# A two-layer hybrid model on one core: tokens by their place in chunks of four, u by block transposes, S5 states as the stationary operand

## The chip, the cores and the metric

One core of a Trainium2 chip runs the whole program; seven are idle. The metric is device time in microseconds of one execution, from 1187.76 us (median of three) for the kernel before. The engines meant below are TensorE (PE, with its weight loads PEld), VectorE (DVE), ScalarE (ACT), GpSimd (POOL) and SyncE (SP), whose queue issues the transfers.

## What is computed

Two layers over 256 tokens of width 1024, float32. Each layer is a half-weighted SwiGLU feed-forward, a mixing stage, and a second feed-forward:

```python
for l in range(DEPTH):
    x = x + 0.5 * swiglu(rms_norm(x, norm_ffn1[l]), ffn1_wi[l], ffn1_wo[l])
    h = rms_norm(x, norm_mix[l])
    (u, q_raw, k_cmp, v_cmp, k_sel, v_sel, k_win, v_win,
     nsa_gate, gate_a, gate_b) = jnp.split(h @ w_in[l], SPLIT_POINTS, axis=-1)
    y_a = s5_branch(u, ...)
    y_b = nsa_branch(q_raw, k_cmp, ...) @ nsa_w_up[l]
    merged = jax.nn.sigmoid(gate_a) * y_a + jax.nn.sigmoid(gate_b) * y_b
    x = x + merged @ w_out[l]
    x = x + 0.5 * swiglu(rms_norm(x, norm_ffn2[l]), ffn2_wi[l], ffn2_wo[l])
```

`s5_branch` is a complex linear recurrence over time in 32 groups of 64 states with 16 inputs and outputs each, then a gelu and a gated projection. `nsa_branch` is attention with eight heads in two key groups, over keys that are compressed (windows of 32 tokens, step 16, through a small network), selected and local; at 256 tokens all blocks are selected.

## The kernel before

Tokens stand on the partitions, 128 in each of two tiles t. The float32 weights come through a ring of four `raw` buffers on SP's queue, in the order of `plan`; ACT rounds each chunk to a high part `whi` (L157, L337), DVE computes the rest `wlo` (L158, L337), and PE multiplies three times for each product (`mm3`, L369 to L371: high by high, high by low, low by high). `gemm` does this for 128x512, 384 or 408 columns, chunk by chunk for both tiles; its results are the tiles `gu`. The smaller products are plain float32.

The mixing stage (`mix`) computes u (512 columns of w_in), then 384 columns (`kvT`, part of the keys), 408 columns (more keys, values, gates), the compression of keys and values (`compress`), q, and the gate columns. Beside it runs a generator, `s5_main`, which `pull` advances by a budget whenever `next` fetches a chunk; `attn_units` follows in it. S5 works in chunks of four tokens: U4 holds for each pair of groups the inputs of a chunk, 4 places × 32 channels on the partitions and 64 chunks along the free axis. Products with G (L538, through `mm_cols`) give each chunk's contribution, `rotate` and a scan (L885, DVE) run the recurrence over 64 chunks and leave the states `Sp`, and L903 adds K·U4 and the two C·Sp to the output, which is passed through gelu (L907) and split.

U4 is made like this: u is evicted by ACT (L1271), turned by four PE transposes per tile (L1274), copied out of PSUM (L1275, ACT) into `uT`, and rearranged by sixteen copies of 32 partitions, half on ACT (L868), half on DVE (L870). The weights of the compression stand in `raw` without a split and are the stationary operand; its input `kc2` is read with a step of eight (L538 from `compress`); POOL fills `kc2` (L530, `gcopy`). The compressed key is normalized and rotated on ACT, DVE and POOL between L1091 (its product) and L1096 (`kb`), which PE transposes at L1103.

The order of the instructions on each engine is written by a scheduler at build time, with its own estimates of durations; `issue_after` and `keep_in_program_order` bind some of it. Engines take their instructions strictly in that order.

The kernel's last step (`finish`, L381) adds each half tile of y to x on DVE and stores it with one transfer of SP's queue.

Of the kernel before, what the change touches and what calls it, by code (L numbers as in the profile page):

```python
# [8 lines left out]
F32R = mybir.dt.float32r  # L9
BF = mybir.dt.bfloat16  # L10
AF = mybir.ActivationFunctionType
# [22 lines left out]


def shape_constants():
    a = np.zeros((128, 128 + CONST_W), np.float32)
    a[:, :128] = np.eye(128)
# [12 lines left out]

    c, s = cs(np.arange(SEQ))
    put('cos', c.reshape(2, 128, 64).transpose(1, 0, 2))
    put('sin', s.reshape(2, 128, 64).transpose(1, 0, 2))
# [6 lines left out]
    put('any', (t >= 31).astype(np.float32).reshape(2, 128).T)  # L61
# [7 lines left out]
    put('caus', np.where(r[None, :] > r[:, None], np.float32(-1e30), np.float32(0)).astype(np.float32))  # L69
    cm = np.where((cend[None, :] <= t[:, None]) & (n[None, :] < 15), np.float32(0), np.float32(-1e30))  # L70
    put('cmask', cm.reshape(2, 128, 16).transpose(1, 0, 2).astype(np.float32))
    return a


class Model:
# [32 lines left out]
    def add(k, ap, split=True, g=None):  # L108

        k.chunks.append((ap, split, g))  # L110

    def load(k, o, i):
# [743 lines left out]

    def s5_main(k, uT):

        nc, P = k.nc, k.P
        V, S = nc.vector, nc.scalar  # L860
        r4 = lambda dt=F32: k.sb([128, 1024], "r4", k.opt['n4'], dt)
        U4 = r4().rearrange("p (a j) -> p a j", a=16)
        for q in range(4):
            for u in range(4):
                o = U4[u * 32:(u + 1) * 32].rearrange("p (a q) j -> p q a j", q=4)[:, q]
                i = uT[q * 32:(q + 1) * 32].rearrange("p a (j u) -> p u a j", u=4)[:, u]
                if u % 2 == 0:
# [23 lines left out]
        for h in range(2):  # L891
            yield from k.rotate(Sp, Z, P['cs'], P['sn'], slice(h * 8, h * 8 + 8), -1)
        yt = r4().rearrange("p (a t s) -> p a t s", a=4, s=4)
# [15 lines left out]
        yh, yl = r4(F32R), r4(F32R)  # L909
        k.split(yt.rearrange("p a t s -> p (a t s)"), yh, yl)  # L910
        k.yT = [t.rearrange("p (a t) -> p a t", a=4) for t in (yh, yl)]
        yield 1.0

# [41 lines left out]
    def nsa_prep(k, l):  # L955
# [21 lines left out]
        N['cg'], N['sg'], N['cc'] = cg, sg, cc  # L977
        kc2 = k.sb([128, 2, 3, 128], "kc2", 1)
        nc.gpsimd.memset(kc2[:, :, 2], 0.0)
        bk = k.bank((128, 32))  # L980
        nc.tensor.transpose(bk, N['pe'], k.id[:32, :32])
        V.tensor_copy(kc2[:, :, 2, 0:16], bk.rearrange("p (a b) -> p a b", a=2))
        N['kc2'] = kc2
# [84 lines left out]
    def compress(k, kvT):  # L1068
# [4 lines left out]
        for kv in range(2):  # L1073
            for h in range(2):
                for a in range(2):
                    i = kvT[h * 64:(h + 1) * 64, kv].rearrange("p (j a) -> p a j", a=2)[:, a]
                    k.gcopy(kc2[a * 64:(a + 1) * 64, kv, h], i)
        hid = k.sb([128, 2, 2, 16], "hid", 1)
        nc.gpsimd.memset(hid[:, :, :, 15:16], 0.0)
        for kv in range(2):  # L1080
            ps = k.bank((128, 3, 15), 'ya')
            for m in range(16):
                if m % 8 == 0:
                    w = k.next().rearrange("p (m c) -> p m c", m=8)
                k.mm_cols(ps, [(w[:, m % 8], kc2[:, kv, :, m:m + 113:8])], m == 0, m == 15)
            pb = k.sb([128, 1], "pb", 2)
            V.tensor_copy(pb, ps[:, 2, 0:1])
            S.activation(hid[:, kv, :, 0:15], ps[:, 0:2], AF.Gelu_apprx_tanh, bias=pb)

# [162 lines left out]
    def mix(k):  # L1252
# [15 lines left out]
        uT = r4().rearrange("p (a t) -> p a t", a=4)  # L1268
# [154 lines left out]
```

## Time and profile before

| what | value |
|---|---|
| median of three runs (lowest, highest) | 1187.76 us (1186.48, 1188.71) |
| the profiled execution | 1188.25 us |
| its span | 1186.4 us |
| PE busy | 1161.3 us (98%), 6724 instructions |
| DVE, ACT, POOL busy | 839.6, 674.6, 231.8 us |
| mean granted clock | 0.996 of 2.4 GHz |

The span runs from the first to the last instruction; the execution's own time adds what lies around it. A busy PE is not PE at its peak: matmuls overlap, a 128x512 one is shown with some 0.39 us and the next begins about 0.23 us later. So unit prices are taken from the starts of successive rows, not from the durations shown.

### The profile page before, as it was taken

To read this page: it belongs to the slowest core of one execution; us is meant where nothing else is said; L and a number is where in the kernel's file an instruction comes from. 1 tells how busy PE (TensorE), PEld (TensorE's weight loads), DVE (VectorE), ACT (ScalarE), POOL (GpSimd) and SP (SyncE) were. 2 spreads that over 40 slices of the span, in tenths; PEclk is the share of its full clock that TensorE was granted. 3 is DMA by queue.
4 is the path that set the end of the run, shared out by engine and by line. 5 is a ranking of instruction groups with operands and counts; after the bars stand their busy time and mean duration, and the time that the engine had idled before them with its cause. 6 is when DMAs were issued, how large, how long until landed. Compare 5 with 4: busy or idle time off the path is not lost. (4 is left out here: it accounts for less than half of the span.)

```text
span 1186.4 us, 18796 instructions
## 1 busy us (share of the span) xinstructions
PE 1161.3 (98%) x6724; PEld 944.9 (80%) x6724; DVE 839.6 (71%) x1494; ACT 674.6 (57%) x1176; POOL 231.8 (20%) x285
## 2 busy tenths in 40 slices
PE   9999999999999999999999999999999999999998
PEld 6888777887877888888888887778778778888886
DVE  5797979586875755555667987886878756655554
ACT  6655554745765565554566555546657646655552
POOL 3002654044032000000030043711341310000000
PEclk9999999999999999999999999999999999999999
DMA  8766555364443566565565656445635435665662
GB/s 237 226 194 184 170 154 179 105 192 144 145 140 104 165 211 187 185 190 183 187 188 178 195 162 182 142 152 155 199 107 173 129 107 160 214 185 188 188 185 89
DMA packets 150078, 200.48 MB, mean 169 GB/s; under 512 B 9952, under 2 KB 120832, under 8 KB 149984
## 3 DMA queue, kind: packets, MB, share of 16 engines
q1 hardware_dynamic: 148848, 197.46, 54.3%
q0 software_dynamic: 1136, 1.82, 0.9%
q8 instruction: 53, 0.87, 0.3%
q14 instruction: 41, 0.34, 0.1%
HBM read 198.18 MB, written 1.05 MB: 168 GB/s over the span
## 5 line engine op out<-in xcount | busy, mean ns | idle before, releaser
L158 DVE SCALAR_TENSOR_TENSOR wlo<-raw,gcol,whi 128x512 fp32r<-128x512 f32 (+2 forms) x480 | 359.0, 785 | 110.0 <-ACT whi L157 107.6
L157 ACT ACTIVATE whi<-raw,gcol 128x512 fp32r<-128x512 f32 (+2 forms) x480 | 316.1, 710 | 193.0 <-PE gu L370 92.4
L369 PE MATMUL gu<-whi,hh 128*128 128x512 f32 (+2 forms) x944 | 372.2, 394 | 0.6 <-ACT whi L157 0.6
L371 PE MATMUL gu<-wlo,hh 128*128 128x512 f32 (+2 forms) x944 | 369.1, 396 | 2.3 <-DVE wlo L158 2.3
L370 PE MATMUL gu<-whi,hl 128*128 128x512 f32 (+2 forms) x944 | 368.9, 391 | 0.0
L337 DVE TENSOR_TENSOR wlo<-raw,whi 128x1024 fp32r<-128x1024 f32 x128 | 160.9, 1259 | 103.1 <-ACT whi L337 101.1
L337 ACT CAST whi<-raw 128x1024 fp32r<-128x1024 f32 x128 | 134.5, 1053 | 135.4 <-PE gu L370 112.1
L371 PEld LDWEIGHTS gu<-wlo,hh 128*128 128x128 f32 x944 | 177.8, 189 | 37.8 <-DVE wlo L158 2.6
L370 PEld LDWEIGHTS gu<-whi,hl 128*128 128x128 f32 x944 | 178.2, 189 | 35.2
L369 PEld LDWEIGHTS gu<-whi,hh 128*128 128x128 f32 x944 | 178.3, 189 | 34.5 <-ACT whi L157 0.8
L344 POOL TENSOR_SCALAR rs<-ss 128x1 f32<-128x1 f32 (+3 forms) x22 | 7.2, 328 | 378.4 <-ACT w2k L351 351.6
L370 PE MATMUL yb<-whi,w1k 128*128 128x512 f32 x176 | 71.4, 406 | 0.7 <-DVE w1k L337 0.7
L371 PE MATMUL yb<-wlo,w1k 128*128 128x512 f32 x176 | 69.2, 393 | 0.0
L369 PE MATMUL yb<-whi,w1k 128*128 128x512 f32 x176 | 69.0, 395 | 0.0
L370 PE MATMUL ya<-whi,w1k 128*128 128x512 f32 x176 | 68.8, 391 | 0.0
L371 PE MATMUL ya<-wlo,w1k 128*128 128x512 f32 x176 | 68.7, 391 | 0.0
L369 PE MATMUL ya<-whi,w1k 128*128 128x512 f32 x176 | 68.2, 393 | 0.0
L1207 POOL TENSOR_SCALAR w2k<-w2k,sm 128x128 f32<-128x128 f32 (+1 forms) x64 | 38.9, 629 | 100.6 <-ACT w2k L1191 63.2
L337 ACT CAST w1k<-tr 128x256 fp32r<-128x256 f32 x88 | 32.5, 370 | 45.7 <-PE tr L484 45.7
L501 DVE SCALAR_TENSOR_TENSOR w1k<-gu,rs,w1k 128x256 f32<-128x256 f32 x88 | 42.0, 479 | 16.2 <-ACT w1k L500 16.2
L500 ACT ACTIVATE w1k<-gu,rs 128x256 f32<-128x256 f32 x88 | 40.9, 467 | 20.0 <-PE gu L371 13.7
L337 DVE TENSOR_TENSOR w1k<-tr,w1k 128x256 fp32r<-128x256 f32 x88 | 36.7, 418 | 10.1 <-ACT w1k L337 10.0
(316 smaller groups left out, 1502.1 us busy)
## 6 DMA issues: line engine op xcount, KB each, us to landing
raw<-in_ffn_wi_dram SPq DMA_DIRECT2D x352, 256.0 KB, 3.3
raw<-in_ffn_wo_dram SPq DMA_DIRECT2D x88, 512.0 KB, 3.6
raw<-in_w_in_dram SPq DMA_DIRECT2D x48, 512.0 KB, 4.5
raw<-in_ssm_w_glu_dram SPq DMA_DIRECT2D x32, 256.0 KB, 3.4
raw<-in_w_out_dram SPq DMA_DIRECT2D x16, 512.0 KB, 3.3
raw<-in_cmp_w_dram SPq DMA_DIRECT2D x8, 512.0 KB, 4.8
raw<-in_nsa_w_up_dram SPq DMA_DIRECT2D x16, 256.0 KB, 4.1
raw<-in_w_in_dram SPq DMA_DIRECT2D x8, 408.0 KB, 4.2
```

Of the source, the lines that this page charges most:

```text
L157: k.hi_ins[i] = k.nc.scalar.activation(hi[:, s], r[:, s], AF.Copy, scale=c)
L158: k.lo_ins = k.nc.vector.scalar_tensor_tensor(lo[:, s], r[:, s], c, hi[:, s].bitcast(F32), op0=ALU.mult, op1=ALU.subtract)
L337: return k.nc.scalar.copy(hi, src), k.nc.vector.tensor_sub(lo, src, hi.bitcast(F32))
L344: k.nc.gpsimd.tensor_scalar(a, ss, scale, EPS, op0=ALU.mult, op1=ALU.add)
L369: mm(ps, a[0], b[0], start=first, stop=False)
L370: mm(ps, a[1], b[0], start=False, stop=False)
L371: return mm(ps, a[0], b[1], start=False, stop=last)
L500: m = nc.scalar.activation(sg, ps[t][:, :256], AF.Silu, scale=r[t])
L501: nc.vector.scalar_tensor_tensor(a, ps[t][:, 256:], r[t], sg, op0=ALU.mult, op1=ALU.mult)
L1207: G.tensor_scalar(w[:, i], p[:, i], cf[:, j:j + 1], 0.0, op0=ALU.mult, op1=ALU.add)
```

## The change

The host lays the tokens of each tile of 128 out by their place in a chunk of four: partition p holds token 4 (p mod 32) + p div 32. Tables and masks are laid out likewise, and the output is stored back in four transfers per half tile, two on SP's queue and two on ACT's. U4 then comes from u by 32x32 block transposes on DVE, one for each tile (L1280 of the changed kernel). The last step of S5 takes the states and U4 as the stationary operand and K and C as the moving one; its output has chunks on the partitions and is transposed back by PE after the gelu (L913). `kc2` is laid out with the eight offsets outermost, and its 33 columns (16 and 16 windows, and the offset's one) are read in order.

```diff
+PLACE = 4 * (np.arange(128) % 32) + np.arange(128) // 32
...
+    def store(k, t, h, xs):
+
+        for u in range(4):
+            o = bass.AP(tensor=k.out.tensor, offset=k.out.offset + (t * 128 + u) * D + h * 512,
+                        ap=[[4 * D, 32], [1, 512]])
+            (k.nc.sync if u % 2 else k.nc.scalar).dma_start(o, xs[u * 32:(u + 1) * 32])
...
-                    k.nc.sync.dma_start(k.out[0, t * 128:(t + 1) * 128, h * 512:(h + 1) * 512], xs)
+                    k.store(t, h, xs)
...
-    def s5_main(k, uT):
+    def s5_main(k, U4):
...
-        U4 = r4().rearrange("p (a j) -> p a j", a=16)
-        for q in range(4):
-            for u in range(4):
-                o = U4[u * 32:(u + 1) * 32].rearrange("p (a q) j -> p q a j", q=4)[:, q]
-                i = uT[q * 32:(q + 1) * 32].rearrange("p a (j u) -> p u a j", u=4)[:, u]
-                if u % 2 == 0:
-                    S.copy(o, i)
-                else:
-                    V.tensor_copy(o, i)
-            yield 0.7
...
-        T = ((P['K'], U4), (P['C'][0], Sp[0]), (P['C'][1], Sp[1]))
+        yh, yl = r4(F32R), r4(F32R)
+
+        T = ((U4, P['K']), (Sp[0], P['C'][0]), (Sp[1], P['C'][1]))
         for h in range(2):
-            bk = k.bank((128, 2, 4, 64), 'yb')
-            for i, (m, v) in enumerate(T):
-                for a in range(2):
-                    for s in range(4):
-                        for q in range(4):
-                            p = h * 8 + a * 4 + q
-                            nc.tensor.matmul(bk[q * 32:(q + 1) * 32, a, s], m[:, p, s * 32:(s + 1) * 32], v[:, p],
-                                             start=(i == 0 and a == 0 and s == 0), stop=(i == 2),
-                                             skip_group_check=True)
-                    yield 0.4
-            S.activation(yt[:, h * 2:h * 2 + 2].rearrange("p a t s -> p a s t"), bk, AF.Gelu_apprx_tanh)
+            bk = k.bank((128, 4, 128), 'yb')
+            for q in range(4):
+                for i, (v, m) in enumerate(T):
+                    for e in range(2):
+                        p = (2 * h + e) * 4 + q
+                        nc.tensor.matmul(bk[e * 64:(e + 1) * 64, q], v[:, p], m[:, p], start=(q == 0 and i == 0),
+                                         stop=(i == 2), skip_group_check=True)
+                yield 0.6
+            g = k.sb([128, 4, 4, 32], "w2k", k.opt['n2'])
+            S.activation(g.rearrange("p s q c -> p q s c"), bk.rearrange("p q (s c) -> p q s c", s=4),
+                         AF.Gelu_apprx_tanh)
             yield 0.6
...
+            bk = k.bank((128, 4, 128))
+            for s in range(4):
+                nc.tensor.transpose(bk[:, s], g[:, s].rearrange("p q c -> p (q c)"), k.id)
+            o = [y.rearrange("p (a s j) -> p s a j", a=8, s=4)[:, :, 4 * h:4 * h + 4] for y in (yh, yl)]
+            k.split(bk.rearrange("p s (a j) -> p s a j", a=4), *o)
...
-                    i = kvT[h * 64:(h + 1) * 64, kv].rearrange("p (j a) -> p a j", a=2)[:, a]
-                    k.gcopy(kc2[a * 64:(a + 1) * 64, kv, h], i)
+                    i = kvT[h * 64:(h + 1) * 64, kv].rearrange("p (n m a) -> p a m n", m=8, a=2)[:, a]
+                    k.gcopy(kc2[a * 64:(a + 1) * 64, kv, :, h * 16:(h + 1) * 16], i)
...
-            ps = k.bank((128, 3, 15), 'ya')
+            ps = k.bank((128, 33), 'ya')
...
-                k.mm_cols(ps, [(w[:, m % 8], kc2[:, kv, :, m:m + 113:8])], m == 0, m == 15)
+                k.mm_cols(ps, [(w[:, m % 8], kc2[:, kv, m % 8, m // 8:m // 8 + 33])], m == 0, m == 15)
...
-            u = k.sb([128, 512], "w2k", k.opt['n2'])
-            S.activation(u, ps[t], AF.Copy, scale=k.r[t])
-            bk = k.bank((128, 4, 128))
-            for i in range(4):
-                nc.tensor.transpose(bk[:, i], u[:, i * 128:(i + 1) * 128], k.id)
-            S.copy(uT[:, :, t * 128:(t + 1) * 128], bk)
-        k.bg, k.budget = k.s5_main(uT), k.opt['B1']
+            u = k.sb([128, 16, 32], "w2k", k.opt['n2'])
+            S.activation(u.rearrange("p a c -> p (a c)"), ps[t], AF.Copy, scale=k.r[t])
+            V.transpose(U4[:, :, t * 32:(t + 1) * 32], u)
+        k.bg, k.budget = k.s5_main(U4), k.opt['B1']
...
-            S.copy(kvT[:, :, t * 128:(t + 1) * 128], bk)
+            for i in range(2):
+                S.copy(kvT[:, i, t * 128:(t + 1) * 128].rearrange("p (j u) -> p u j", u=4),
+                       bk[:, i].rearrange("p (u j) -> p u j", u=4))
```

In the changed kernel most lines stand 5 to 13 lower: L538 becomes L550, L903 L904, L907 L908, L1091 L1098, L1096 L1103, L1103 L1110. The scheduler's order changes in the two mixing stages alone, but for the copies that fill `kc2`'s last column. Three places of layer 1 follow.

ACT from the eviction of u's first half (L1271 before, L1279 now) to the eviction of the 384-column product (L1282 before). Before:

```order
L1271 ACTIVATE w2k<-gu,rs 128x512
L157 ACTIVATE whi<-raw,gcol 128x384 x4
L1271 ACTIVATE w2k<-gu,rs 128x512
L1275 COPY r_8212<-tr 128x4x128 x2
L868 COPY r_8239<-r_8212 32x4x64 x6
L157 ACTIVATE whi<-raw,gcol 128x408 x2
L868 COPY r_8239<-r_8212 32x4x64 x2
L157 ACTIVATE whi<-raw,gcol 128x408 x4
```

Now:

```order
L1279 ACTIVATE w2k<-gu,rs 128x512
L169 ACTIVATE whi<-raw,gcol 128x384 x4
L1279 ACTIVATE w2k<-gu,rs 128x512
L169 ACTIVATE whi<-raw,gcol 128x408 x6
L1287 ACTIVATE w1k<-gu,rs 128x256
L1289 ACTIVATE kp<-gu,rs 128x128
```

All copies between the second half of u and the 408-column splits are gone.

PE at the compression of layer 1 (`kc` is its input). Of the names before, r_8239 is U4 and r_7571 is K; of those of the change, r_8056 is U4, r_8522 and r_8523 are the two Sp, r_7415 is K, r_7427 and r_7428 are the two C. The last name of a pair is the stationary operand. Before:

```order
L538 MATMUL yb<-r_8239,r_7376 64x64 x15
L538 MATMUL ya<-kc_7745,raw 64x45 x64
L903 MATMUL yb<-r_8239,r_7571 32x64 x9
L369 MATMUL gu<-whi,hh 128x512
L370 MATMUL gu<-whi,hl 128x512
L369 MATMUL gu<-whi,hh 128x512
L370 MATMUL gu<-whi,hl 128x512
L903 MATMUL yb<-r_8239,r_7571 32x64 x26
```

Now:

```order
L550 MATMUL ya<-kc_7589,raw 64x33 x64
L904 MATMUL yb<-r_7415,r_8056 64x128 x2
L904 MATMUL yb<-r_7427,r_8522 64x128 x2
L904 MATMUL yb<-r_7415,r_8056 64x128
L904 MATMUL yb<-r_7428,r_8523 64x128 x2
L904 MATMUL yb<-r_7415,r_8056 64x128
L381 MATMUL gu<-whi,hh 128x512
L382 MATMUL gu<-whi,hl 128x512
L381 MATMUL gu<-whi,hh 128x512
L382 MATMUL gu<-whi,hl 128x512
L904 MATMUL yb<-r_7415,r_8056 64x128
L904 MATMUL yb<-r_7427,r_8522 64x128 x2
```

Before, K·U4 alone stood here, and the products with Sp only 48 gemm matmuls later; now products with both Sp stand ahead of q's first gemm matmuls.

DVE at the compressed key (kc, then kb) of layer 1. Before:

```order
L997 TENSOR_TENSOR nr_8678<-tr,rs 32x64
L999 TENSOR_TENSOR nr_8680<-nr_8678,cc 32x64
L158 SCALAR_TENSOR_TENSOR wlo<-raw,gcol,whi 128x512 x2
L1059 TENSOR_TENSOR w2k<-w2k,rs 128x512
L1005 TENSOR_TENSOR kc<-nr_8680,nr_8681 32x64
L158 SCALAR_TENSOR_TENSOR wlo<-raw,gcol,whi 128x512 x2
L1061 TENSOR_TENSOR w2k<-w2k,cg 128x512
L1096 COPY kb<-kc 32x128
L158 SCALAR_TENSOR_TENSOR wlo<-raw,gcol,whi 128x512 x3
```

Now:

```order
L1004 TENSOR_TENSOR nr_8500<-tr,rs 32x64
L1006 TENSOR_TENSOR nr_8502<-nr_8500,cc 32x64
L349 TENSOR_TENSOR kT<-tr,kT 64x2x128
L1066 TENSOR_TENSOR w2k<-w2k,rs 128x512
L1012 TENSOR_TENSOR kc<-nr_8502,nr_8503 32x64
L1068 TENSOR_TENSOR w2k<-w2k,cg 128x512
L1103 COPY kb<-kc 32x128
L1119 TENSOR_TENSOR vc<-tr,cst 128x512
L349 TENSOR_TENSOR kct<-tr,kct 128x2x16
L1073 TENSOR_TENSOR w2k<-w2k 128x4x64 x2
```

Two splits between kc and kb are gone, and of the two ahead of kc as well. On PE, 24 gemm matmuls stood between the products L1091 and the transpose L1103 that needs kb; now 24 stand between L1098 and L1110 in layer 0, and 20 in layer 1, with nine and three matmuls of L904 beside them.

## Rows read from the trace of the kernel before

**Rows 1.** part 1 of the page, busy time, share of the span and instructions of each engine

```profile
PE 1161.3 (98%) x6724; PEld 944.9 (80%) x6724; DVE 839.6 (71%) x1494; ACT 674.6 (57%) x1176; POOL 231.8 (20%) x285
```

**Rows 2.** PE's waits, whole span: us in total, times, longest us

```profile
PE ya L538 <- ACT r L868: 3.3, 2, 1.6
PE tr L1103 <- DVE kb L1096: 3.2, 2, 1.6
PE gu L371 <- DVE wlo L158: 2.3, 2, 1.4
PE yb L903 <- issue: 1.2, 1, 1.2
PE tr L1287 <- ACT w1k L1282: 1.0, 2, 0.5
PE gu L369 <- ACT whi L157: 0.6, 1, 0.6
```

**Rows 3.** busy time by stretch: PE, PEld, DVE, ACT, POOL, granted clock, DMA share, GB/s

```profile
280.00:290.00 10.00, 8.39 (x31) 6.49 (x30) 8.71 (x15) 6.93 (x12) 8.13 (x5) 0.83 0.54 150
810.00:820.00 10.00, 8.37 (x82) 7.94 (x82) 4.25 (x10) 7.13 (x12) 0.13 (x1) 1.00 0.22 69
870.00:880.00 10.00, 8.37 (x32) 6.51 (x31) 7.19 (x14) 3.31 (x8) 6.28 (x4) 0.83 0.68 203
```

**Rows 4.** groups by line: busy us, mean ns of one | idle before, releaser

```profile
L903 PE MATMUL yb<-r,r 128*32 128x64 f32 x768 | 17.6, 222 | 1.2 <-issue 1.2
L584 DVE TENSOR_TENSOR r<-w2k 128x512 f32<-128x512 f32 x8 | 8.4, 1054 | 1.7 <-POOL w2k L582 1.7
```

**Rows 5.** timeline, ACT, layer 1: start, us, engine, line, operation [idle before]

```profile
808.63 0.67 ACT L1271 ACTIVATE w2k<-gu,rs 128x512 f32<-128x512 f32 x1
813.28 3.96 ACT L868 COPY r<-r 32x256 f32<-32x256 f32 x6
```

**Rows 6.** timeline, PE, layer 1's mixing stage

```profile
807.59 0.60 PE L1274 MATMUL tr<-id,w2k 128*128 128x128 f32 x4
808.38 0.34 PE L371 MATMUL gu<-wlo,hh 128*128 128x384 f32 x1
808.56 0.34 PE L369 MATMUL gu<-whi,hh 128*128 128x384 f32 x1
...
819.79 1.39 PE L538 MATMUL ya<-r,r 128*64 128x64 f32 x40 [1.63 <-ACT r L868]
...
860.46 0.40 PE L370 MATMUL gu<-whi,hl 128*128 128x512 f32 x1
860.79 0.30 PE L903 MATMUL yb<-r,r 128*32 128x64 f32 x2
...
861.36 0.39 PE L369 MATMUL gu<-whi,hh 128*128 128x512 f32 x1
...
895.53 2.33 PE L903 MATMUL yb<-r,r 128*32 128x64 f32 x152
...
959.20 1.96 PE L1228 MATMUL yb<-w2k,V 128*64 128x128 f32 x30
```

**Rows 7.** timeline, DVE, layer 1's mixing stage

```profile
824.27 0.68 DVE L925 TENSOR_TENSOR w2k<-ya,r 128x512 f32<-128x512 f32 x1
...
826.66 0.68 DVE L925 TENSOR_TENSOR w2k<-yb,r 128x512 f32<-128x512 f32 x1
...
836.94 2.47 DVE L885 TENSOR_TENSOR_SCAN r<-r,r 128x1024 f32<-128x1024 f32 x1
...
842.07 0.72 DVE L158 SCALAR_TENSOR_TENSOR wlo<-raw,gcol,whi 128x512 fp32r<-128x512 f32 x1
```

**Rows 8.** timeline, PE, compression of layer 1

```profile
833.28 5.60 PE L538 MATMUL ya<-kc,raw 128*64 128x45 f32 x127
```

**Rows 9.** line 381, the stores: issue ns min/median/max, and landing

```profile
L381 SPq DMA_DIRECT2D out_dram<-x x4: 332/338/347, 1179.0 to 1182.9; - x4
DMA to landing us min/median/max: 2.0/2.0/2.0
```

More of the change, by code (lines that the diff above doesn't have):

```diff
@@ L33 @@
 CONST_W = _o
+PLACE = 4 * (np.arange(128) % 32) + np.arange(128) // 32
 def shape_constants():
     a = np.zeros((128, 128 + CONST_W), np.float32)
+    tok = PLACE
     a[:, :128] = np.eye(128)
@@ L52, in shape_constants @@
     c, s = cs(np.arange(SEQ))
-    put('cos', c.reshape(2, 128, 64).transpose(1, 0, 2))
-    put('sin', s.reshape(2, 128, 64).transpose(1, 0, 2))
+    put('cos', c.reshape(2, 128, 64)[:, tok].transpose(1, 0, 2))
+    put('sin', s.reshape(2, 128, 64)[:, tok].transpose(1, 0, 2))
     n = np.arange(16)
@@ L60, in shape_constants @@
     t = np.arange(SEQ)
-    put('any', (t >= 31).astype(np.float32).reshape(2, 128).T)
+    put('any', (t >= 31).astype(np.float32).reshape(2, 128)[:, tok].T)
     r = np.arange(128)
@@ L68, in shape_constants @@
     put('i32', (r[:, None] % 32 == np.arange(32)[None, :]).astype(np.float32))
-    put('caus', np.where(r[None, :] > r[:, None], np.float32(-1e30), np.float32(0)).astype(np.float32))
+    put('caus', np.where(tok[None, :] > tok[:, None], np.float32(-1e30), np.float32(0)).astype(np.float32))
     cm = np.where((cend[None, :] <= t[:, None]) & (n[None, :] < 15), np.float32(0), np.float32(-1e30))
-    put('cmask', cm.reshape(2, 128, 16).transpose(1, 0, 2).astype(np.float32))
+    put('cmask', cm.reshape(2, 128, 16)[:, tok].transpose(1, 0, 2).astype(np.float32))
     return a
@@ L892, in s5_main @@
             yield from k.rotate(Sp, Z, P['cs'], P['sn'], slice(h * 8, h * 8 + 8), -1)
-        yt = r4().rearrange("p (a t s) -> p a t s", a=4, s=4)
-        T = ((P['K'], U4), (P['C'][0], Sp[0]), (P['C'][1], Sp[1]))
+        yh, yl = r4(F32R), r4(F32R)
+        T = ((U4, P['K']), (Sp[0], P['C'][0]), (Sp[1], P['C'][1]))
         for h in range(2):
-            bk = k.bank((128, 2, 4, 64), 'yb')
-            for i, (m, v) in enumerate(T):
-                for a in range(2):
-                    for s in range(4):
-                        for q in range(4):
-                            p = h * 8 + a * 4 + q
-                            nc.tensor.matmul(bk[q * 32:(q + 1) * 32, a, s], m[:, p, s * 32:(s + 1) * 32], v[:, p],
-                                             start=(i == 0 and a == 0 and s == 0), stop=(i == 2),
-                                             skip_group_check=True)
-                    yield 0.4
-            S.activation(yt[:, h * 2:h * 2 + 2].rearrange("p a t s -> p a s t"), bk, AF.Gelu_apprx_tanh)
-            yield 0.6
-        yh, yl = r4(F32R), r4(F32R)
-        k.split(yt.rearrange("p a t s -> p (a t s)"), yh, yl)
+            bk = k.bank((128, 4, 128), 'yb')
[9 more added lines that the diff above has]
+                         AF.Gelu_apprx_tanh)
+            yield 0.6
+            bk = k.bank((128, 4, 128))
[3 more added lines that the diff above has]
+            k.split(bk.rearrange("p s (a j) -> p s a j", a=4), *o)
+            yield 0.8
         k.yT = [t.rearrange("p (a t) -> p a t", a=4) for t in (yh, yl)]
-        yield 1.0
     def rotate(k, out, x, cs, sn, sl, sign):
@@ L977, in nsa_prep @@
         N['cg'], N['sg'], N['cc'] = cg, sg, cc
-        kc2 = k.sb([128, 2, 3, 128], "kc2", 1)
-        nc.gpsimd.memset(kc2[:, :, 2], 0.0)
+        kc2 = k.sb([128, 2, 8, 34], "kc2", 1)
         bk = k.bank((128, 32))
         nc.tensor.transpose(bk, N['pe'], k.id[:32, :32])
-        V.tensor_copy(kc2[:, :, 2, 0:16], bk.rearrange("p (a b) -> p a b", a=2))
+        for kv in range(2):
+            V.tensor_copy(kc2[:, kv, :, 32:34], bk[:, kv * 16:(kv + 1) * 16].rearrange("p (i m) -> p m i", i=2))
         N['kc2'] = kc2
@@ L1084, in compress @@
                     w = k.next().rearrange("p (m c) -> p m c", m=8)
-                k.mm_cols(ps, [(w[:, m % 8], kc2[:, kv, :, m:m + 113:8])], m == 0, m == 15)
+                k.mm_cols(ps, [(w[:, m % 8], kc2[:, kv, m % 8, m // 8:m // 8 + 33])], m == 0, m == 15)
             pb = k.sb([128, 1], "pb", 2)
-            V.tensor_copy(pb, ps[:, 2, 0:1])
-            S.activation(hid[:, kv, :, 0:15], ps[:, 0:2], AF.Gelu_apprx_tanh, bias=pb)
+            V.tensor_copy(pb, ps[:, 32:33])
+            S.activation(hid[:, kv, :, 0:15], ps[:, 0:32].rearrange("p (h n) -> p h n", h=2)[:, :, 0:15], AF.Gelu_apprx_tanh, bias=pb)
         pk = k.bank((32, 64))
@@ L1267, in mix @@
             k.rh.append(w)
-        uT = r4().rearrange("p (a t) -> p a t", a=4)
+        U4 = r4().rearrange("p (a j) -> p a j", a=16)
         for t in range(2):
-            u = k.sb([128, 512], "w2k", k.opt['n2'])
-            S.activation(u, ps[t], AF.Copy, scale=k.r[t])
-            bk = k.bank((128, 4, 128))
-            for i in range(4):
-                nc.tensor.transpose(bk[:, i], u[:, i * 128:(i + 1) * 128], k.id)
-            S.copy(uT[:, :, t * 128:(t + 1) * 128], bk)
-        k.bg, k.budget = k.s5_main(uT), k.opt['B1']
+            u = k.sb([128, 16, 32], "w2k", k.opt['n2'])
+            S.activation(u.rearrange("p a c -> p (a c)"), ps[t], AF.Copy, scale=k.r[t])
+            V.transpose(U4[:, :, t * 32:(t + 1) * 32], u)
+        k.bg, k.budget = k.s5_main(U4), k.opt['B1']
         ps = k.gemm(k.hstat, 8, 384)
@@ L1413 @@
     data = {n: np.ascontiguousarray(inputs[n]) for n in _INS}
+    data['x'] = np.ascontiguousarray(data['x'].reshape(1, SEQ // 128, 128, D)[:, :, PLACE].reshape(1, SEQ, D))
     data['consts'] = shape_constants()
```

## Prediction

> **What bounds the kernel now.** I read the page first: TensorE (PE) is busy 98% of the span [rows 1]. So the time is the sum of three things: what PE executes, what it waits, and what a low clock costs it. A cut on another engine counts only where PE waited for that engine. Of PE's waits [rows 2] those of the two mixing stages, which the change rewrites, add to 11.6 us: 3.3 us for S5's input (L538 for the copies of L868), 1.0 us for `w1k` of L1282 in the same place, 2.9 us for the first splits of the q chunk (L371, L369), 3.2 us for the compressed key (L1103 for `kb`), 1.2 us of issue at L903. The third view, busy time and clock by stretch [rows 3], shows that the wait for `kb` is paid twice: in the 10 us around each of the two the granted clock averages 0.83, between 1.2 and 2.4 GHz, so some 10 × 0.17 = 1.7 us more go in each layer. The timeline then gives unit prices.
>
> **u without TensorE.** Removed per layer: two blocks of four transposes, two ACT copies, eight ACT copies, six of them in 3.96 us, and eight DVE copies [rows 5]. What PE feels is their place: from 813.28 the copies hold ACT, U4 is complete at 819.8, and PE, which has nothing else in its order, stands 1.63 us before L538 [rows 6]. The 408-column splits queue behind the copies on ACT, and `w1k` behind those. In the new order ACT goes straight from L1279 to the splits; U4 is two DVE transposes. No row shows that operation. From below I take the nearest plain 128x512 DVE work, 2.39 us for four, 0.60 each [rows 7]; from above half a 128x1024 scan, 1.2 us. ACT evicts u's second half by 809.3 [rows 5], so U4 is there at 810 to 811, while PE reaches its first S5 matmul 34 gemm matmuls of 0.175 us after 807.6 [rows 6], at 813.5. Three microseconds cover it, so the price is zero at either end. Both waits go: **-4.3 us** for two layers. If ACT were late again, part of the 1.0 would stay.
>
> **Compression.** L538 read 45 columns with a step of eight; now it reads 33 adjacent ones. Before, 127 instructions take 5.60 us, 44 ns each [rows 8]; S5's L538, the same 128x64 weights with 64 adjacent columns, takes (1.39 - 0.22)/39 = 30 ns [rows 6]. More columns in less time, so columns do not set the 44. I take 30: 256 × 14 ns = **-3.6 us**. Bounds: nothing, if the 44 has another cause, and 30 × 33/64 = 15 ns, -7.4. The Trainium skill, "SBUF — State Buffer", in its paragraph on cachelines, says that fp32 reads stepping over more than four elements pay for a new line each time; by it the step is the cause and the sum below holds; if the 44 had another cause, the sum would be -9.7. No row separates the step from the rest. The rearranging moves to the copies that fill `kc2`, eight on POOL and four, not two, on ACT. Taken at the 0.66 us of L868's [rows 5] they are 8 us, and PE has the 408-column gemm, 48 × 0.187 = 9 us, to hide them; without it the excess over 9 would be PE's.
>
> **States stationary.** 384 instructions per layer (a plain fp32 matmul is two in the trace, 768 for 2 × 192 [rows 4]) of 32 weight columns, at (2.33 - 0.22)/151 = 14 ns, become 96 of 64 weight columns and 128 moving ones, at (1.96 - 0.28)/29 = 58 ns [rows 6], the price of L1228. That is 5.4 against 5.6 us: nothing. What moves is the number of places where plain fp32 interrupts the gemm stream. One such place with a single matmul costs 861.36 - 860.46 - 2 × 0.23 = 0.44 us [rows 6], 0.4 without its content. Counting in both orders, all such blocks of the program fall from 208 to 202: 6 × 0.4 = 2.4. **-2.4 us**. Sixteen transposes of the output replace sixteen of u: nothing. Bounds: 0, if the regrouping gives nothing; -4.8, if each of the six places fewer with an L903 per layer (twelve before, six with L904) saved its 0.4.
>
> **The new wait.** Before, the K·U4 products, which need no state, came first behind the compression; now the order puts C·Sp there already with the third matmul. If DVE isn't there yet, PE waits, and everything behind it in PE's order too. PE's arrival: 807.6 + 48 × 0.175 + 128 × 0.030 (S5) + 4 × 0.4 (blocks) + 0.4 (transposes) + 48 × 0.187 (408 columns, by columns) = 830.8; compression 3.8 to 5.6 and its block 0.4: 835 to 837. DVE: S5's first bank is done 64 × 0.030 after 813.5, at 815.4; then twenty 128x512 operations at 0.60, two scans of 2.4, six 408-column splits at no more than that [rows 7], small ones 0.5, and 1 us waiting for S5's second bank: 837.3. So PE waits 0.3 to 2.3 us per layer, 1.3 in the middle, 2.6 in all. In its place the 2.9 us for the q chunk's splits go, for DVE reaches them at 839 to 840 instead of 842.07 [rows 7] while PE still works off what it has. Together **0**, bounds -2.9 and +1.7.
>
> **The compressed key.** `kb` hangs on a chain PE, ACT, DVE, POOL, DVE from L1091 (now L1098). Before, PE had 24 gemm matmuls and a little S5 work under it, 6.2 us, and waited 1.6: the chain took 7.8. In DVE's new order two splits of 0.7 us no longer stand between kc and kb, so I put it at 6.4. Layer 0 now has 24 gemm matmuls and nine S5 ones (two instructions each) under it, 24 × 0.23 + 9 × 0.11 + 3 × 0.4 = 7.7: no wait, and no dip. Layer 1 has 20 and three, 5.3: the wait stays at about 1.1, and I leave its dip. **-3.3 us** (1.6 + 1.7). Bounds: 0 if nothing is gained (-0.7 if the chain keeps its 7.8: layer 0's wait goes, layer 1's grows by 0.9, both dips stay); -6.6 if both waits and both dips go. Elsewhere a wait just as long, 1.63 us at 819.79 [rows 6], left the clock at 1.00 [rows 3], so I give no dip to other waits.
>
> **Issue, store.** The 1.2 us of issue came in one layer only, in a burst of 14 ns instructions; I take nothing, bound -1.2. The last half tile leaves as four transfers of 64 KB, two on each of two queues, rather than one; earlier ones have a microsecond each. One issue takes 0.338 us, landing 2.0 [rows 9]. If an issue keeps its price the second on a queue starts 0.34 later: **+0.3**. Bounds 0 (issue shrinks with the partitions) and +2.0 (they land one after the other). The Trainium skill, "DMA: Bandwidth & Descriptors", Rules for kernel authors, speaks against this part: transfers on disjoint partitions serialize, since they share the same engines. By it the term would be its upper bound and the sum below -11.6. No row here shows two small stores at once.
>
> **Sum.** -4.3 - 3.6 - 2.4 + 0 - 3.3 + 0.3 = -13.3. The profiled execution took 1188.25 us (span 1186.4), 0.5 above the median of 1187.76. 1188.25 - 13.3 = 1174.9; I say **1175.0 us**.
>
> **Rivals.**
> (a) *Half of it.* U4's waits go (-4.3) and 2.4 of blocks, but the 44 ns stay, PE waits 2.3 for the states in both layers (+1.7), both dips remain, +0.3: -4.7, 1183.5. For it: DVE is full from 840 on in the old trace, and the new order gives the states no slack. Against: same weights at 30 ns are in the trace.
> (b) *All of it.* As forecast, and layer 1's kb wait goes with its dip, and the issue wait too: -13.3 - 3.3 - 1.2 = -17.8, 1170.5.
> (c) *Slower: the states on DVE become the bound.* Each 128x512 operation with POOL running beside it took 1.05 us [rows 4], not 0.60. If all twenty ran so, PE would wait 20 × 0.45 = 9 us more per layer: -13.3 + 18 = +4.7, 1193.0. It decides from 13.3/2 = 6.7 us per layer, 0.33 us on each operation. Against: in that stretch the new order gives POOL only the key copies and two memsets until the reductions.
> (d) *It does nothing*, since work only changes engines: the transposes of u return as transposes of the output, and a wait of DVE's comes for each removed one (+4.3 + 2.4 + 3.3 given back): -3.3 at most of compression, or 0 if that is 44 ns too: 1185 to 1188, say 1187.
>
> **Chances.** Forecast 0.55, (a) 0.19, (b) 0.12, (c) 0.07, (d) 0.07. A difference under 0.2% (2.4 us) cannot be told from none. Faster: forecast, (a), (b): 0.86; same 0.06; slower 0.08, (d) being split. The range reaches from (b) with a further 2.5 us of compression's bound, 1168, to (a) and a landing 0.5 late, 1184: what is left out is (c), (d) and the tails of (a) and (b), below 0.2.
>
> **What would show it.** Right: no PE wait for a copy of u and 1.6 us less before S5's first matmuls; compression's instructions at 30 ns or below; L904 in six-odd blocks per layer; a wait of PE for DVE's L933 or L938 of 1 to 2 us right behind the compression; the clock whole around layer 0's kb and below 1 around layer 1's. Wrong: compression still at 44 ns; waits for L938 above 3 us; a clock dip at a new place; the end of the span more than 1 us later behind the last DVE add than before.

## The result: 1180.72 us, and the profile after

The changed kernel took **1180.72 us** (median of four, 1180.34 to 1181.57) against 1187.6 for the kernel before (median of four: the three behind 1187.76 and one more): ratio 0.9943, 95% interval 0.9929 to 0.9958. It is faster, inside the range, and 5.7 us above the forecast of 1175.0. The profiled execution took 1180.87 us, its span 1179.1.

Part 1 of the page after, which answers to [rows 1]:

```profile
PE 1155.5 (98%) x6148; PEld 941.3 (80%) x6148; DVE 840.6 (71%) x1486; ACT 661.5 (56%) x1162; POOL 213.4 (18%) x283
```

PE's waits after, which answer to [rows 2]: us in total, times, longest us.

```profile
PE tr L1110 <- DVE kb L1103: 3.8, 2, 3.3
PE yb L904 <- DVE r L933: 3.1, 2, 1.6
...
PE gu L381 <- ACT w2k L1046: 1.2, 2, 1.1
PE tr L1098 <- PE yb L904: 0.9, 1, 0.9
...
PE tr L1032 <- DVE w1k L1012: 0.6, 1, 0.6
```

The waits for u's copies, for `w1k` of L1282, for q's splits and for issue are gone. The wait for `kb` has stayed (all but 0.49 us of it in layer 1), the predicted wait for Sp (`r` of L933) has come, and the mixing stages have three small new ones. Busy time and clock by stretch, columns as in [rows 3]:

```profile
250.00:260.00 10.00, 9.72 (x49) 7.51 (x50) 8.83 (x19) 8.12 (x15) 5.43 (x6) 0.83 0.75 228
270.00:280.00 10.00, 9.51 (x42) 6.98 (x43) 6.48 (x13) 3.98 (x9) 5.42 (x8) 0.83 0.36 105
830.00:840.00 10.00, 8.45 (x104) 6.62 (x101) 9.46 (x21) 5.56 (x10) 3.69 (x4) 0.83 0.81 257
860.00:870.00 10.00, 9.33 (x37) 7.66 (x38) 7.78 (x14) 7.21 (x12) 3.98 (x5) 0.83 0.26 70
```

Two stretches had a granted clock of 0.83 in the profiled execution before; in this one there are four. Each costs 10 × 0.17 = 1.7 us. The new ones, at 250 and 830, stand at the wait for Sp. PE's timeline in layer 1 shows it, behind the compression (`kc`), which answers to [rows 8]:

```profile
827.89 3.92 PE L550 MATMUL ya<-kc,raw 128*64 128x33 f32 x128
...
831.65 0.42 PE L904 MATMUL yb<-r,r 128*64 128x128 f32 x4
833.62 1.92 PE L904 MATMUL yb<-r,r 128*64 128x128 f32 x12 [1.55 <-DVE r L933]
835.46 0.80 PE L381 MATMUL gu<-whi,hh 128*128 128x512 f32 x1
```

The compression's 128 instructions fell from 5.60 to 3.92 us, 31 ns each. Two products of K·U4 (four instructions) follow, then PE stands 1.55 us. q's first matmul behind is shown with 0.80 us, where 0.39 is usual: the lower clock.

An account of the span, used for every kernel below: PE's busy time, the rest of the span (waits, head and tail), and the clock's part of the busy time, which is the sum of 10 us × (1 - granted clock) over the ten-us stretches up to 1160. The last overlaps a wait at times, so it is good to a microsecond or two.

| | forecast | measured (before, after) |
|---|---|---|
| PE's busy time without the clock's part | -3.6 - 2.4 = -6.0 | 1157.9 to 1148.7: -9.2 |
| rest of the span | -4.3 - 1.6 + 0.3 = -5.6 | 25.1 to 23.6: -1.5 |
| the clock's part | -1.7 | 3.4 to 6.8: +3.4 |
| sum | -13.3 | -7.3 |

PE was given less work, as forecast and more. It waits nearly as long as before and loses twice as much to the clock.

### The profile page after: what moved, and what is told of

The parts are those of the page before. It is cut to its first block, busy times and chain, and to the rows that moved or that the text cites. A ratio compares the mean times of both kernels' runs of the same rounds, so it can differ in the third digit from the quotient of the medians.

```text
span 1179.1 us, 17646 instructions
## 1 busy us (share of the span) xinstructions
PE 1155.5 (98%) x6148; PEld 941.3 (80%) x6148; DVE 840.6 (71%) x1486; ACT 661.5 (56%) x1162; POOL 213.4 (18%) x283
## 3 DMA queue, kind: packets, MB, share of 16 engines
HBM read 198.18 MB, written 1.05 MB: 169 GB/s over the span
## 4 chain that ended last, share of the span: by engine, by line
PE 88%; DVE 5%; POOL 3%; issue 1%; ACT 1%; DMA 0%; SPq 0%; DVEq 0%; ACTq 0%; POOLq 0%
PE gu L381 18%; PE gu L383 18%; PE gu L382 18%; PE ya L383 4%; PE yb L381 4%; PE ya L381 4%; PE yb L382 4%; PE yb L383 4%; PE ya L382 4%; DVE wlo L170 2%; POOL r L542 2%; PE tr L496 2%; PE yb L1235 1%; PE tr L375 1%; PE gu L448 1%
## 5 line engine op out<-in xcount | busy, mean ns | idle before, releaser
L1214 POOL TENSOR_SCALAR w2k<-w2k,sm 128x128 f32<-128x128 f32 (+1 forms) x64 | 31.6, 514 | 113.0 <-DVE sm L1206 52.1
```

The costliest lines, as they stand in the source:

```text
L1214: G.tensor_scalar(w[:, i], p[:, i], cf[:, j:j + 1], 0.0, op0=ALU.mult, op1=ALU.add)
```

## The experiments

The first theory: each part has its price on PE, the parts add up, and what was missing went into the waits for Sp and `kb` and into the clock behind them. The second, formed after the first four runs: the moment at which Sp and the next weight tile are ready is fixed by other engines, so what PE saves in front of it comes back as waiting. The kernels of the twelve experiments were timed in three groups, each beside the kernel before, whose median there was 1187.27, 1187.98 or 1187.16 us; so medians of different groups compare to about 0.8 us. The last three columns are from one profiled execution each, and the clock's part differs between executions of one kernel (last section). "Kb later" and "K first" are edits explained below.

| kernel | median us | ratio to before, 95% interval | PE busy | rest | clock |
|---|---|---|---|---|---|
| before | 1187.6 | | 1161.3 | 25.1 | 3.4 |
| changed | 1180.72 | 0.9943 (0.9929 to 0.9958) | 1155.5 | 23.6 | 6.8 |
| compression alone | 1191.19 | 1.0029 (1.0017 to 1.0040) | 1162.1 | 27.7 | 6.9 |
| u and stores alone | 1173.10 | 0.9881 (0.9868 to 0.9895) | 1156.3 | 14.7 | 0 |
| u, compression (old states) | 1178.35 | 0.9933 (0.9921 to 0.9946) | 1157.0 | 22.3 | 3.4 |
| u, states (old compression) | 1174.08 | 0.9891 (0.9877 to 0.9904) | 1153.5 | 18.7 | 0 |
| changed, K first | 1177.87 | 0.9913 (0.9900 to 0.9926) | 1155.6 | 22.1 | 3.4 |
| changed, kb later | 1175.25 | 0.9897 (0.9884 to 0.9911) | 1154.3 | 19.1 | 3.4 |
| changed, both | 1171.12 | 0.9861 (0.9847 to 0.9874) | 1150.3 | 18.8 | 0 |
| **both, old compression** | **1169.21** | 0.9848 (0.9835 to 0.9862) | 1153.3 | 13.9 | 0 |
| kb later, fewer `w1k` | 1174.67 | 0.9890 (0.9877 to 0.9904) | 1155.1 | 18.5 | 3.4 |
| kb later, five `raw` | 1176.79 | 0.9911 (0.9898 to 0.9925) | 1158.0 | 18.5 | 3.4 |
| kb later, old states | 1182.25 | 0.9959 (0.9945 to 0.9972) | 1155.4 | 23.4 | 0 |
| before, kb later | 1195.56 | 1.0075 (1.0062 to 1.0087) | 1160.3 | 33.1 | 1.7 |

Any edit makes the scheduler write a new order, and not only at the edit. So a kernel's time is that of its edit together with its order.

### The parts apart

**Compression alone**, in the kernel before:

```diff
-        kc2 = k.sb([128, 2, 3, 128], "kc2", 1)
+        kc2 = k.sb([128, 2, 8, 34], "kc2", 1)
...
-                k.mm_cols(ps, [(w[:, m % 8], kc2[:, kv, :, m:m + 113:8])], m == 0, m == 15)
+                k.mm_cols(ps, [(w[:, m % 8], kc2[:, kv, m % 8, m // 8:m // 8 + 33])], m == 0, m == 15)
```

> The kernel before with one part of the change alone: the compression's copies and products in the new layout (33 contiguous columns in place of 45 strided ones). Theory (the products' price falls from 44 to 30 ns each, 256 of them, all on TensorE's path): 1183.6 to 1184.6 us, 3 to 4 below the kernel before, with an advance of TensorE of 3.9 per 128 kc products. Rival (the copies into the new layout are slower on GpSimd and the compression's chain ends later, so kb comes late and gives it back): 1187 to 1189, with the same cheap products but kb's wait grown by 3 or more.

3.9 us slower than the 1187.27 beside it: past the rival, and for another reason than `kb`. The products fell to 31 ns. PE's waits:

```profile
PE gu L369 <- ACT whi L157: 3.5, 2, 2.0
...
PE gu L371 <- DVE wlo L158: 2.2, 1, 2.2
PE tr L1103 <- DVE kb L1096: 1.6, 1, 1.6
```

and PE's timeline behind the compression of layer 1:

```profile
839.92 0.52 PE L903 MATMUL yb<-r,r 128*32 128x64 f32 x18
842.41 0.80 PE L369 MATMUL gu<-whi,hh 128*128 128x512 f32 x1 [1.97 <-ACT whi L157]
843.01 0.63 PE L370 MATMUL gu<-whi,hl 128*128 128x512 f32 x1
```

The 1.7 us saved per layer ends in front of q's first operand: `whi` in both layers (1.57 and 1.97 us), in layer 0 with 2.17 us for `wlo` behind it. The clock falls below 1 behind these waits in both layers.

**u and the stores alone**: the changed kernel with the compression's lines turned back (as above, - and + exchanged) and with the states' products as before (their loops, the gelu and the split behind them too):

```diff
-        T = ((U4, P['K']), (Sp[0], P['C'][0]), (Sp[1], P['C'][1]))
+        T = ((P['K'], U4), (P['C'][0], Sp[0]), (P['C'][1], Sp[1]))
...
```

> The kernel before with the tokens by place, u by block transposes and the four stores alone; compression in the old layout (45 strided columns) and the states' products with K and C as weights. First theory (the parts add up, each with its own price on TensorE): u's two waits of 1.6 and w1k's of 0.5 go, 1183 to 1184 us. Second theory (which waits are left, and how long each one is in one piece, decides; u's early end moves the whole states' chain on VectorE forward, and with the long old compression the next weight tile is there in time): below the kernel with u and the short compression (1178.35), 1174 to 1178. Rival (u saves its own wait and makes kb or y late): 1186 to 1189.

14.1 us below the kernel before, below either theory's range. PE's waits in the mixing stages are these (the others are older than the change):

```profile
PE gu L381 <- ACT whi L169: 0.5, 1, 0.5
PE tr L1108 <- DVE kb L1101: 0.4, 2, 0.2
PE gu L383 <- DVE wlo L170: 0.2, 1, 0.2
```

Against [rows 2], the waits for `r`, `w1k` and issue are gone, `kb` fell from 3.2 to 0.4 and q's splits from 2.9 to 0.7. No stretch lies below full clock. The rest of the span fell by 10.4 us, the clock's part by 3.4, PE's other work by 1.6.

**u and compression**, with the old states' products:

> The changed kernel with the states' products turned back: K and C moving out of the weights' side again (weights K and C, 64 columns of U4 and Sp moving, two activations and one split behind them); token layout, block transposes, compression and stores stay as changed. Theory (states stationary is worth 5 us of TensorE's work, by fewer interruptions, but has cost 3.1 of waits for Sp and 3.4 of dips): about 1179 to 1182 us, within 2 of the changed kernel, with the wait for y or Sp smaller and TensorE's busy time larger by 2 to 5. First rival (states stationary is worth its whole 5 us, waits and dips are there either way): 1184 to 1187. Second rival (it is a loss by itself): 1174 to 1177.

1178.35, between the ranges, 2.4 below the changed kernel and 5.3 above u alone. The wait for Sp is gone and one for `whi` stands in its place, 1.47 and 2.44 us.

**u and states**, with the old compression:

> The changed kernel with the compression in the old layout. First theory (the products' saving of 3.7 us is real whatever stands behind): 1184 to 1185 us. Second theory (the saved time is spent waiting behind the compression for Sp or for the next weight tile, and the clock falls there): 1178 to 1181, the waits for Sp gone and one or two stretches at the lower clock with them, and so no slower than the changed kernel.

1174.08: 6.6 us faster than the changed kernel, though its compression costs PE more. The second theory gave the direction, and too little of it. PE's timeline at the place of the 1.55 us wait:

```profile
824.41 5.58 PE L550 MATMUL ya<-kc,raw 128*64 128x45 f32 x128
829.81 1.29 PE L904 MATMUL yb<-r,r 128*64 128x128 f32 x16
```

and VectorE's, with the Sp that the products wait for; first of this kernel, then of the changed one:

```profile
828.98 0.67 DVE L933 TENSOR_TENSOR r<-w2k 128x504 f32<-128x504 f32 x1
```

```profile
832.89 0.67 DVE L933 TENSOR_TENSOR r<-w2k 128x504 f32<-128x504 f32 x1
```

Sp is ready 5.2 us after the compression's start here (829.65 - 824.41), 5.7 us in the changed kernel (833.56 - 827.89). A compression of 5.58 us ends when Sp is there; one of 3.92 us ends 1.75 us early, of which the two products of K·U4 leave a wait of 1.55. Of the rest, the wait for `kb` is as in the changed kernel (4.2 against 3.8), but no stretch is below full clock:

```profile
860.00:870.00 10.00, 9.12 (x43) 7.60 (x44) 7.27 (x14) 4.53 (x9) 6.27 (x5) 1.00 0.57 159
```

### The waits taken away

**K first**: the eight products of each half that need no state go ahead of the others.

```diff
-            for q in range(4):
-                for i, (v, m) in enumerate(T):
+            for i, (v, m) in enumerate(T):
+                for q in range(4):
...
-                yield 0.6
+                yield 0.8
```

> The changed kernel, with the eight products of K and U4 of each half issued ahead of all products of the states (outer loop over the terms, inner over q). Theory (the changed kernel's new waits of 1.5 us for Sp, one per layer, and the two stretches at the lower clock that come behind them, take back 3.1 + 3.4 us): both go, 1174 to 1177 us, and the ten-us stretches round 250 and 830 show a granted clock of 1.00. First rival (the dips come from the many short fp32 products themselves, not from the wait): the waits go, the clock still falls, 1177 to 1179. Second rival (whatever stands ahead, TensorE only meets the next late thing, a split operand or y): 1180 to 1182 with the wait moved to another tile.

1177.87, in the first rival's range, but by the second rival's mechanism: the wait for Sp went, and `whi` (3.2) and `wlo` (0.7) came. In layer 0 the idle time is as long as the old wait, in two pieces, 0.89 and 0.70, and the clock stays whole (1.00 from 250 to 260). In layer 1 it is one piece of 2.32, and the clock falls (0.83 from 830 to 840). So the short products don't pull the clock down by themselves. Two of this kernel's five executions, with a mean granted clock of 1.000, took 1175.1 and 1175.2 us, which is the theory's range; the three with 0.997 took 1177.9 to 1179.5. The other fall left (890 to 900) stands behind a wait of 2.28 us for `r` of L1319; by its new order this kernel has no wait for `kb`.

**Kb later**: `compress2`, with the transpose of `kb`, is bound behind the last matmul of the first gate `gemm`, no longer behind that of q's.

```diff
-        with k.tc.issue_after(k.mm.ins):
-            k.compress2(*cm)
...
                 ps = k.gemm(k.hstat, 8, 512)
+                if d is ta and c == 0:
+                    with k.tc.issue_after(k.mm.ins):
+                        k.compress2(*cm)
```

> The changed kernel, with the second half of the compression and with it kb put behind one more gate product group (issued behind the first gate product in place of before it). Theory (kb's chain over DVE is what TensorE waits for, 3.8 us, with one dip of 1.7 us per layer behind it): kb's waits and both dips go, 1173 to 1176 us. Rival (the gate products' own operands or the later reader of kb then wait, so the idle time only moves): 1179 to 1182 with the sum of TensorE's waits within 1 us of the changed kernel's.

1175.25, 5.5 below the changed kernel, as the theory said: no wait for `kb`, rest -4.5, two of four falls of the clock gone.

**Both edits.**

> The changed kernel with both edits: K and U4 products first, and the second half of the compression one gate product group later. First theory (each edit takes away a wait of its own, and TensorE's work is all that is left): 1169 to 1172 us. Second theory (behind the compression TensorE cannot go on anyhow, since the next weight tile is only loaded when the first of the four compression tiles is used up, and its split operand comes some 3 us after the last compression product; with K first, that wait shows as one for whi, 1.6 in layer 0 and 2.3 in layer 1, as in the kernel with K first alone): 1174 to 1177, no better than with the later kb alone (1175.25).

1171.12, inside the first theory's range. The waits for `whi` and `wlo` are there as the second said (2.8 in all), but in pieces of 0.90 at most; the longest wait in the mixing stages is 1.36 us. Against "kb later" alone the rest of the span hardly moved (19.1 to 18.8) and PE's busy time fell by 4.0, of which 3.4 is the clock. The stretches that were at 0.83:

```profile
250.00:260.00 10.00, 8.75 (x44) 6.33 (x43) 8.80 (x18) 8.30 (x16) 4.96 (x6) 1.00 0.74 228
830.00:840.00 10.00, 9.76 (x58) 7.37 (x57) 9.74 (x20) 8.41 (x16) 4.87 (x5) 1.00 0.75 237
```

**Both, with the old compression.**

> The kernel with K and U4 products first and the later kb, with the compression in the old layout: what the new layout is worth where the clock no longer falls. First theory (3.7 us of TensorE's work, all on its path): 1174 to 1175.5 us, against 1171.1. Second theory (the waits for whi and wlo behind the compression, 2.8 in all, shrink by most of what it takes longer): 1171.5 to 1173.

1169.21, the lowest median, 1.9 below the same kernel with the new layout; both theories expected it slower. The two ran in different groups and the intervals of their ratios overlap, so the difference itself is not resolved; the 3 to 4 us of the first theory are excluded. PE's busy time is 3.0 higher and the rest 4.9 lower. All of PE's waits:

```profile
PE tr L496 <- DVE w1k L513: 2.9, 2, 1.4
PE tr L823 <- DVE w1k L349: 2.9, 2, 1.4
PE ya L300 <- POOL w1k L294: 1.7, 1, 1.7
PE gu L448 <- ACT hh L349: 0.7, 1, 0.7
PE yb L382 <- DVE w1k L349: 0.7, 2, 0.3
PE tr L375 <- DVE x L391: 0.2, 1, 0.2
```

None lies in the mixing stages.

### The load, the states, and kb in the kernel before

**Five `raw` buffers**, paid for with three of the tag `w1k`, and beside it the control with the fewer `w1k` alone:

```diff
-OPT = dict(nr=4, nh=4, LA=2, DLA=3, n1=10, n2=8, ...)
+OPT = dict(nr=5, nh=4, LA=2, DLA=3, n1=7, n2=8, ...)
```

The reason to try it: the four compression tiles fill the ring. In the changed kernel SP issues the load of q's first tile 1.17 us after the compression's start, and ACT's first split of it waits for that transfer:

```profile
829.06 10.74 SPq L125 DMA_DIRECT2D raw<-in_w_in_dram  x6
```

```profile
834.41 1.34 ACT L169 ACTIVATE whi<-raw,gcol 128x512 fp32r<-128x512 f32 x2 [5.51 <-DMA raw<-in_w_in_dram]
```

Layer 0 shows both layouts side by side: load and first split of the changed kernel, whose compression starts at 244.56, then of u and states with the old compression, which starts at 244.61.

```profile
245.73 3.17 SPq L125 DMA_DIRECT2D raw<-in_w_in_dram  x4
249.46 1.34 ACT L169 ACTIVATE whi<-raw,gcol 128x512 fp32r<-128x512 f32 x2 [3.88 <-DMA raw<-in_w_in_dram]
```

```profile
246.20 4.45 SPq L125 DMA_DIRECT2D raw<-in_w_in_dram  x4
249.81 1.33 ACT L169 ACTIVATE whi<-raw,gcol 128x512 fp32r<-128x512 f32 x2 [4.19 <-DMA raw<-in_w_in_dram]
```

The new layout ends the compression 1.7 us earlier, but q's operand is there only 0.35 us earlier: the load needs the buffer of the first compression tile alone, and is issued 1.2 us after the compression's start against 1.6. In all kernels with four buffers q's first matmul starts 5.60 to 7.65 us after the compression's start with the new layout, 6.05 to 6.71 with the old.

> The kernel with the later kb, with five raw weight buffers in place of four (paid for in memory by 7 in place of 10 buffers of the tag w1k), so that one gate weight tile is loaded while the four compression tiles are in the ring. Second theory (the load behind the compression is what TensorE waits for in this place): the load of the next gate weights lands before the last compression product, TensorE goes on with gate products there, the Sp wait (1.6 per layer) and its dip go: 1170 to 1173 us. Rival (Sp comes late from VectorE whatever is loaded): 1174.5 to 1176. What the fewer w1k buffers cost is seen from the kernel with these alone, run beside it.

> Control for the five raw buffers: the kernel with the later kb, with four raw buffers as before and 7 in place of 10 buffers of the tag w1k. Both theories: 1174.5 to 1178 us, the cost of the fewer buffers alone, if there is any.

The control cost nothing (1174.67). With five buffers 1176.79: the second theory's number failed, its mechanism held one step further. q's first matmul now follows the compression at once (3.86 us after its start, in both layers), the wait for Sp is gone, and the keys' operand is what PE meets next. PE's waits with five buffers:

```profile
PE tr L1032 <- DVE w1k L1012: 5.4, 2, 3.2
...
PE gu L381 <- ACT whi L169: 1.0, 2, 0.7
```

The rest of the span is 18.5 us in both kernels; with five buffers PE's busy time is 2.9 us higher, in another order. The load decides when q starts; for the whole time it was one of several late things.

**Old states' products, kb later.**

> The kernel with the later kb and the old states' products (weights K and C stationary), so that the states' part of the change is weighed where kb no longer disturbs. First theory (states stationary is worth 5 us of TensorE's work and costs a wait for Sp and its dip): 1176 to 1179 us, slower than the 1175.25 of the later kb by 1 to 4. Second theory (the work that it saves stands in front of waits for loads and splits and comes back as waiting): 1174 to 1176, no difference.

1182.25, slower than either range and 7.0 above "kb later" with the new states (its profiled execution, 1180.54, is the fastest of five). So there the states' part is worth 7.0 us. Against "both", the other kernel of the new layout without a fall of the clock, PE is 5.1 us busier. The groups by line, busy us and mean ns, of this kernel and then of "both":

```profile
L905 PE MATMUL yb<-r,r 128*32 128x64 f32 x768 | 17.8, 222 | 0.0
```

```profile
L904 PE MATMUL yb<-r,r 128*64 128x128 f32 x192 | 13.9, 278 | 0.0
```

So states as the stationary operand do save PE's work. In the setting of u and old compression, work fell by 2.8, the wait for `kb` rose from 0.4 to 4.2, and the medians differ by 1.0, which the intervals do not resolve.

**Kb later in the kernel before.**

> The kernel before with the second half of the compression put one gate product group later. Theory (kb's chain over VectorE ends late in both kernels; its two waits of 1.6 us and the two falls of the clock behind them, 3.4, go): 1181 to 1183 us, TensorE's waits for kb gone and no stretch at a granted clock of 0.83. Rival (the edit is worth something only where VectorE was moved by the change): 1186 to 1189.

8.4 us slower than the 1187.16 beside it: the rival, and beyond it. The wait for `kb` and its falls of the clock went, but the order now has these waits of PE:

```profile
PE gu L371 <- DVE wlo L158: 5.5, 4, 1.5
PE tr L1217 <- POOL w2k L1207: 4.1, 2, 2.1
PE gu L369 <- ACT r L1313: 3.6, 2, 1.8
```

"Kb later" is no improvement of its own. It took 5.5 us off the changed kernel and 6.8 off "K first", and cost 3.9 with the old states (1178.35 to 1182.25) and 8.4 here. Which waits the new order brings decides; why it is these was not isolated.

## Why the prediction was right in sign, and where its steps failed

**Right by errors of both signs.** The sum put 13.3 us; 6.9 came, and that it fell inside the range is in part luck. u gave far more than its term, the compression took back most of the surplus, and the clock fell at new places.

**u, -4.3: right in kind, too small.** The U4 transposes take 0.71 us each, between the bounds of 0.60 and 1.2, and delay nobody. But the term counted the two waits at their own place. Alone, u with the stores is worth 14.1 us: the waits for `kb`, q's splits and issue shrink too, and both falls of the clock go. That the freed ScalarE and VectorE and the earlier S5 chain did this is argued; the parts of u were not tried one by one. The prediction spread part of that over "the new wait" and "the compressed key", and left the issue wait at zero.

**Compression, -3.6: the price was right, the path was wrong.** "I take 30: 256 × 14 ns" is what the trace shows, 44 to 31 ns. Weights of the same shape cost 31 with 33 adjacent columns and 30 with S5's 64, so the strided reading, not the number of columns, made the 44. The Trainium skill ("SBUF — State Buffer", paragraph on cachelines) says that each access which crosses to a new line pays a penalty, so that fp32 can be stepped over only so far for free; the trace agrees (44 against 31 ns), though no run changed the step alone. But in no setting did the kernel gain from it. Old to new layout moved the median by +3.9 (in the kernel before), +5.3 (with u), +6.6 (u and states), +1.9 (with both edits, not resolved); PE's work without the clock fell by 2.7 to 4.8, and the rest rose by 2.6 to 7.6. This is the step that failed most: the whole saving was put on PE's path, where q's first operand came only 0.35 us earlier for it (layer 0), and Sp no earlier. The prediction held the numbers to see it: with a compression of 5.6 us PE was to arrive at 837, with VectorE at 837.3; with 3.8 at 835. The microseconds credited under "Compression" are those of "the new wait". They were entered once as a gain, and the wait was set against q's splits, which u alone nearly removed. Why the rest can rise by more than the work falls was not isolated; each new layout also came with a new order.

**States, -2.4: right in kind, at the low end in size.** PE's work without the clock fell by 2.8 with the old compression, 4.9 with the new one and 4.5 with `kb` later. What the kernel got from it was +1.0 (not resolved; the longer wait for `kb` gave it back), +2.4 and -7.0 us.

**The new wait, 0: its length was right, its price was not.** Forecast 1.3 us per layer, measured 1.54 and 1.55. The sentence that failed is "I give no dip to other waits", drawn from one row where a wait of 1.63 us left the clock whole. Both new waits had one: 3.4 us.

**The compressed key, -3.3.** In layer 0 the wait fell to 0.49, as said nearly; in layer 1 it grew to 3.30 where 1.1 was forecast, and both stretches below full clock remained, layer 0's behind other waits (0.88 and 1.05 us, 267 to 270). The term came out near zero.

**Issue and store.** The 1.2 us of issue went, the term's bound. The store's term was nothing: from the start of VectorE's last add to the end of the span 4.26 us before, 4.23 after (1174.87 to 1179.1). The four transfers are issued on two queues:

```profile
L122 SPq DMA_DIRECT2D out_dram<-x x8: 314/384/467, 1171.7 to 1176.0; - x8
L122 ACTq DMA_DIRECT2D out_dram<-x x8: 374/424/452, 1171.7 to 1176.0; - x8
```

The Trainium skill ("DMA: Bandwidth & Descriptors", Rules for kernel authors) has transfers on disjoint partitions serialize, which would have been the bound of +2.0; the measurement does not show that cost.

**The rivals.** (a), half of it, forecast 1183.5, came nearer (2.8 us off, against 5.7) and describes the changed kernel best: PE waiting for the states in both layers and a fall of the clock near both `kb`. It was wrong on the 44 ns. (c) did not come near; VectorE's operations there took 0.67 us.

## What to carry to other kernels

Before crediting a cut, find what the engine meets next and when that is ready; if another engine or a load fixes that moment, the cut is a wait, and here also a fall of the clock. Try the parts of a change apart: here one of them held more than the whole gain, and another gave some 5 us of it back. Where a scheduler rewrites the order at each edit, a part's value holds only in the order it was measured in; the lowest median was that of u and states with K first and `kb` later on the old compression, 1169.21 us.

## What the runs showed of the hardware that was not expected

A wait's length did not tell whether the clock falls. A wait of 1.55 us for Sp had a stretch at 0.83 behind it in both layers of the changed kernel; a wait of 2.08 us for `kb` in the kernel of u and states had none, in either layer:

```profile
860.88 0.21 PE L1110 MATMUL tr<-id,kb 32*128 32x32 f32 x1 [2.08 <-DVE kb L1103]
...
861.59 0.39 PE L382 MATMUL gu<-whi,hl 128*128 128x512 f32 x1
```

Nor did two waits of 0.88 and 1.05 us close together decide: in the changed kernel a fall came behind them, with "kb later" the same two had none. What tells these cases apart is open, and the order of the instructions cannot do it alone: executions of one kernel differ. K first had a mean granted clock of 1.000 in two executions and 0.997 in three, u and compression 0.998 to 1.000 in three (1178.2 to 1178.4 us) and 0.997 and 0.994 in two (1181.1 and 1181.8). The kernel before had 0.998 or 0.999 in 22 of its 29 executions beside the experiments, and 0.996 in the profiled one: its two falls, which the forecast counted on, are more than it usually has. In the profiles the clock's part comes in steps of some 1.7 us; from the changed kernel to both edits it gave 6.8 us and the rest of the span 4.8.

The load of q's first tile in layer 1, issued in the same place, reached ScalarE 5.2 us after its issue with K first (826.54 to 831.75) and 3.8 with both edits (825.09 to 828.86). That is the whole difference between their waits for `whi` there, 2.32 and 0.90.
